# A two-layer token-mixer kernel on one core: preparation distance, bank emptying and bias place in the stage of seven block products

## The chip, the core and the metric

The kernel runs on 1 core of one Trainium2 chip. Its engines are TensorE (PE in the profile, with its weight loads as PEld), VectorE (DVE), ScalarE (ACT), GpSimd (POOL) and SyncE (SP), which issues most DMAs. The metric is device time in microseconds (us) of one launch, here the median of the runs shown.

## The reference

Two layers. In each, h = RMSNorm(x), one wide projection of h feeds four branches (pooling, latent attention, short convolution, attention into memory tokens), each branch is projected back, weighted by a sigmoid gate that also comes from h, and the sum goes through an output projection onto x. All is fp32; the sequence has 256 rows and the model 2048 columns. The stage that the change touches computes these pieces of it:

```
proj = h @ w_in[l]
(pv, pz, cq, ckv, kr, mz, cb, cc, cx, cz, xq, xz, gpre) = jnp.split(proj, split_points, axis=-1)
y_pool = pool_mixer(pv, pool_w[l], pool_scale[l]) * jax.nn.silu(pz)
y_conv = conv_mixer(cb, cc, cx, conv_w[l]) * jax.nn.silu(cz)
gates = jax.nn.sigmoid((gpre + gate_b[l]).astype(jnp.float32)).astype(x.dtype).reshape(B, S, N_BRANCH, D_MODEL)
```

pool_mixer takes causal window means of pv in four groups and multiplies each group by a 256x256 matrix; conv_mixer is cb times a three-tap causal convolution of cc * cx.

## The kernel before

**Number format.** Every fp32 weight is split on the chip into two parts that TensorE takes in one pass each: `hi`, a rounded copy made by ACT, and `lo`, the remainder, a subtraction on DVE. A weight chunk of 128 x 1024 therefore means a DMA into a `raw` tile (4 buffers), a cast into `hi` (5 buffers) and a subtraction into `lo` (5 buffers). The activations were split in the same way earlier (`op` tiles).

**The stage.** In each layer, after the gates of the mla and mem branches and before those of the pool and conv branches, `pool_branch` and `conv_branch` run on "fine" blocks (`fine_block`, L367 on): 128 output features, two weight chunks of 8 row blocks, per chunk 8 matmuls of 512 columns (L376: hi against the activations' hi and lo at once) and 8 of 256 (L379: lo against hi). A block gathers in one bank of PSUM, `ms`, 128 x 512: the main sum in its left half, the part from the activations' lo in its right half. There are two `ms` buffers. `fine_sum` empties the bank: ACT copies the right half into `fmt` (L384), DVE adds left half and copy (L385). There are 48 such blocks a layer; `pool_branch` also has 8 small tiles (L337, L338) of four matmuls, in the same `ms` buffers and emptied by the same `fine_sum`.

**The stream of products.** Between the blocks run three groups a layer of "seven block products" (`seven`, L413 on): a gate projection of 256 rows and 1024 columns done as seven half-size products instead of eight, with sums of weight quarters (L454, L455, L464, L465 on DVE) against sums of activation quarters made earlier (`sx`). A group walks over 8 pairs of row blocks. Each pair loads two `raw` tiles (L444), makes four hi/lo pairs (casts L446, L453, L463, L473; subtractions L438) and issues seven products of three matmuls (L429 to L431). They gather in seven banks: six in three `acc` tiles, the seventh in an `ms` tile that the group holds throughout, so that the blocks have the other `ms` buffer alone. After the last pair, DVE combines the banks (L482 to L489), adds the bias `gate_b` and ACT takes the sigmoid (L491 to L495); the result goes to DRAM as `kept` until `gates` fetches it.

**What interleaves them.** `seven` is a generator that yields after each product. `fine_block` first calls `pull(RATE)`, with RATE = 160/46 = 3.48 owed turns, and each pool tile `pull(1)`; `pull` takes whole turns from the first generator. A turn that gives True (a group is finished) ends the pull. `drain` takes what is left at the stage's end.

**What sets the order.** Instructions are written out in Python; a list scheduler then orders each engine's queue by priority, that is, place of writing, among what its own model of time holds ready, and gives out buffers in that order. `tc.high_priority(AHEAD)` lifts an instruction by 100 places: the DMA, cast and subtraction of a weight chunk then stand ahead of work written up to 100 places earlier. On the chip each engine works through its queue in that fixed order and waits where an input is missing.

Of the kernel before, what the change touches and what calls it, by code (L numbers as in the profile page):

```python
# [14 lines left out]
ALU = mybir.AluOpType  # L15
AX = mybir.AxisListType

P = 128
AHEAD = 100
PB = 2  # L20
D_H, D_MEM, D_LAT, D_XQ, D_MT = 4, 4, 6, 4, 3
SEQUENCE = "A0 A1 F T0 F T1 S0 A2 F V0 T2 S1 A3 F V1 T3 S2 F V2 S3 F V3 X0 X1 F Y0 Y1 X2 X3 F Y2 Y3"
# [4 lines left out]
S = 256  # L27
# [94 lines left out]
def tile_hybrid_trunk(  # L122
# [3 lines left out]
    V, A, T = nc.vector, nc.scalar, nc.tensor  # L126
# [28 lines left out]
    def t2(s):  # L155
        return tp.tile([P, 512], F32, tag="t2", name=nm(s), bufs=7)
# [145 lines left out]
    def defer(runs, delay):  # L302
        if len(background) < delay:
            background.extend([None] * (delay - len(background)))
        background.extend(runs)

    def wchunks(l, name, c0):
        off, n, nk, kt = plan[name, c0]
        m = nk * n
        for k0 in range(0, kt, nk):  # L310
            raw = wp.tile([P, 1024], F32, tag="raw", name=nm("raw"), bufs=4)
            hi = wp.tile([P, 1024], F32R, tag="hi", name=nm("hi"), bufs=5)
            lo = wp.tile([P, 1024], F32R, tag="lo", name=nm("lo"), bufs=5)
            o = off + P * n * k0
            step()
            with tc.high_priority(AHEAD):
                nc.sync.dma_start(raw[:, :m], weights[l, o : o + P * m].rearrange("(p m) -> p m", p=P))
                A.copy(hi[:, :m], raw[:, :m])  # L318
                V.tensor_tensor(lo[:, :m], raw[:, :m], hi[:, :m].bitcast(F32), ALU.subtract)  # L319
            yield k0, nk, kt, n, *(w[:, :m].rearrange("p (k n) -> p k n", n=n) for w in (hi, lo))  # L320
# [29 lines left out]
                    T.matmul(ps[:, j, :S], lo[:, k, n0 : n0 + P], o, start=False, stop=k0 + k == kt - 1)  # L350
        return ps

    stream, owed = [], [0.0]

    def pull(n):
        owed[0] += n
        while stream and owed[0] >= 1:
            owed[0] -= 1
            done = next(stream[0], True)
            if done:  # L360
                stream.pop(0)
                break

    def drain():
        while stream:
            owed[0] = 1000.0
            pull(0)  # L367
        owed[0] = 0.0
# [11 lines left out]
        return ps  # L380

    def fine_sum(dst, ps):
        tmp = t2("fmt")[:, :S]
        A.copy(tmp, ps[:, S:])  # L384
        V.tensor_tensor(dst, ps[:, :S], tmp, ALU.add)  # L385

    def fine_pair(dst, h, l, c0):
        for j in range(2):
# [23 lines left out]
    def seven(l, bi, ep, h, sx):  # L412
# [5 lines left out]
        for u in range(8):  # L418
# [19 lines left out]
                V.tensor_tensor(x[1][:, cols], raw[:, cols], x[0][:, cols].bitcast(F32), ALU.subtract)  # L438

            ra, rb = (wp.tile([P, 1024], F32, tag="raw", name=nm("raw"), bufs=4) for _ in range(2))  # L440
            with tc.high_priority(AHEAD):
                for i, r in enumerate((ra, rb)):
                    at = off + P * 1024 * (2 * u + i)
                    nc.sync.dma_start(r, weights[l, at : at + P * 1024].rearrange("(p m) -> p m", p=P))  # L444
                x = pair()
                A.copy(x[0][:, left], ra[:, left])  # L446
                lower(x, ra, left)
            product(1, "A11", x, left)
            yield False
            both = slice(0, 1024)  # L450
            with tc.high_priority(AHEAD):
                x = pair()
                A.copy(x[0], rb)  # L453
                V.tensor_tensor(ra[:, left], ra[:, right], ra[:, left], ALU.subtract)  # L454
                V.tensor_tensor(ra[:, right], rb[:, right], ra[:, right], ALU.subtract)  # L455
                lower(x, rb, both)
# [1 line left out]
            yield False  # L458
            product(2, "A12", x, left)
            yield False  # L460
            with tc.high_priority(AHEAD):
                x = pair()
                A.copy(x[0], ra)  # L463
                V.tensor_tensor(rb[:, right], rb[:, right], ra[:, left], ALU.subtract)  # L464
                V.tensor_tensor(rb[:, left], rb[:, right], rb[:, left], ALU.subtract)  # L465
                lower(x, ra, both)
# [1 line left out]
            yield False  # L468
            product(7, "S3", x, right)
            yield False  # L470
            with tc.high_priority(AHEAD):
                x = pair()
                A.copy(x[0], rb)  # L473
                lower(x, rb, both)
# [12 lines left out]
        V.tensor_tensor(c, c, bank[5], ALU.add)  # L487
        V.tensor_tensor(g[1][:, 0, :], c, bank[3], ALU.add)
        V.tensor_tensor(g[0][:, 1, :], u3, bank[4], ALU.subtract)  # L489
        for i in range(2):  # L490
            gb = tp.tile([P, 512], F32, tag="gb", name=nm("gb"), bufs=2)  # L491
            nc.sync.dma_start(gb, bcast_rows(gate_b[l, c0 + 512 * i : c0 + 512 * (i + 1)]))
            V.tensor_tensor(g[i], g[i], gb.unsqueeze(1).broadcast_to([P, 2, 512]), ALU.add)
            A.activation(g[i], g[i], AF.Sigmoid)
            nc.gpsimd.dma_start(kept[bi, 2 * ep + i], g[i])  # L495
        yield True

    def fm_sum(dst, ps):
        tmp = t2("fmt").rearrange("p (n s) -> p n s", n=2)
# [92 lines left out]
    def mem_operands(gt):  # L592
# [3 lines left out]
        def get(i):  # L596
            if i not in made:
                f0 = 2 * i
                mt = t2("mt").rearrange("p (k s) -> p k s", k=2)
                made[i] = opnd()  # L600
                with tc.high_priority(AHEAD):
                    if i == 0:
# [119 lines left out]
    def xattn_scores(hd, xq, rq, kT):  # L722
# [6 lines left out]
        for t in range(2):  # L729
            for n in range(2):  # L730
# [3 lines left out]
                )  # L734
        pb = tp.tile([P, 512], F32, tag="pb", name=nm("pb"), bufs=PB)
        softmax_rows(ps, pb, ((0, S), (S, 2 * S)), rq[hd], 2)
# [294 lines left out]
    for l in range(DEPTH):  # L1031
# [51 lines left out]
        flush()  # L1083
        stream += [seven(l, bi, ep, h, sx) for bi, ep in SEVEN]
        owed[0] = -RATE
        y_pool = pool_branch(l, vec, h)
        y_conv = conv_branch(l, vec, h)
        drain()
        gates(l, h, y_pool, "pool", False, False)
        mT = gates(l, h, y_conv, "conv", False, True)  # L1090
        if l + 1 < DEPTH:
# [66 lines left out]
```

## Time and profile before

| what | us |
|---|---|
| median of 3 runs | 2582.64 (2579.9 to 2584.72) |
| the profiled execution's own time | 2583.21 |
| its span | 2581.4 |
| the stage in layer 0 | 629 to 1069 of the span |
| the stage in layer 1 | 1912 to 2353 of the span |

Times in the views count from the start of the span. A matmul's row is longer than its distance to the next one, since matmuls are pipelined; the distance from start to start is what PE needs. In a list of waits, "PEld acc L429 <- ACT hi L446" reads: the weight load of line 429 for `acc` waited for the cast of line 446. The granted clock (PEclk) is TensorE's, 1.00 at full speed.

### The profile page before, as it was taken

Reading aid. Unit: us, or ns where it says so; the run is one execution under the profiler, and the core shown is the slowest. Engines: PE = TensorE matmul, PEld = TensorE weight load, DVE = VectorE, ACT = ScalarE, POOL = GpSimd, SP = SyncE. Lnnn points to the kernel's source line nnn. Section 1 sums busy time; section 2 is a strip of 40 time slices with the busy share of each in tenths; the row PEclk is TensorE's granted clock in tenths of the full one; section 3 lists DMA queues with packets and bytes.
Section 4 is the critical chain, followed back from the end, with each engine's and each line's share of the span. In section 5 each row is a group of like instructions: output and inputs, shape, how many; then the busy total and the mean of one; then the engine's idle time right before and its main releaser. Section 6 shows DMA issues by size and latency. Waiting matters only on the chain.

```text
span 2581.4 us, 33256 instructions
## 1 busy us (share of the span) xinstructions
PE 2511.1 (97%) x12258; PEld 2091.0 (81%) x12258; DVE 1799.0 (70%) x2646; ACT 1338.9 (52%) x1881; POOL 40.5 (2%) x88
## 2 busy tenths in 40 slices
PE   8999999999998999999999999999999999899999
PEld 6888888888877878888888888888888778788887
DVE  6767786556878878766574577965568777777653
ACT  7556674444545455445454566744445454544442
POOL 0000000000000000000000000000000000001000
PEclk9999999999999999999999999999999999999999
DMA  8665436676545565776655653466765455567764
GB/s 310 214 205 164 142 128 222 225 236 219 183 162 187 174 214 189 267 294 232 218 186 162 202 170 123 147 220 226 232 210 188 163 188 193 186 201 273 257 228 147
DMA packets 154052, 522.03 MB, mean 202 GB/s; under 512 B 17312, under 2 KB 18336, under 8 KB 153888
## 3 DMA queue, kind: packets, MB, share of 16 engines
q1 hardware_dynamic: 142800, 481.06, 56.8%
q0 software_dynamic: 10368, 37.75, 4.0%
q8 instruction: 96, 1.57, 0.2%
q10 hardware_dynamic: 720, 1.09, 0.1%
q14 instruction: 68, 0.56, 0.1%
HBM read 496.76 MB, written 23.07 MB: 201 GB/s over the span
## 4 chain that ended last, share of the span: by engine, by line
PE 88%; DVE 6%; DMA 2%; ACT 2%; issue 1%; SPq 0%; DVEq 0%; ACTq 0%
PE acc L333 18%; PE acc L332 18%; PE acc L331 18%; PE ms L376 13%; PE ms L379 6%; PE acc L347 4%; PE acc L350 2%; DVE lo L319 2%; DMA raw<-in_weights_dram 2%; PE acc L430 2%; PE acc L429 2%; PE acc L431 2%; DVE lo L438 1%; ACT hi L318 1%; PE ms L870 1%
## 5 line engine op out<-in xcount | busy, mean ns | idle before, releaser
L319 DVE TENSOR_TENSOR lo<-raw,hi 128x1024 fp32r<-128x1024 f32 (+1 forms) x788 | 942.6, 1199 | 579.7 <-ACT hi L318 572.3
L318 ACT CAST hi<-raw 128x1024 fp32r<-128x1024 f32 (+1 forms) x788 | 812.1, 1033 | 879.9 <-PE acc L333 586.5
L331 PE MATMUL acc<-hi,op 128*128 128x512 f32 (+2 forms) x2112 | 812.5, 385 | 6.0 <-ACT op L555 5.7
L332 PE MATMUL acc<-lo,op 128*128 128x512 f32 (+2 forms) x2112 | 808.0, 383 | 1.6 <-DVE lo L319 1.6
L333 PE MATMUL acc<-hi,op 128*128 128x512 f32 (+2 forms) x2112 | 808.5, 383 | 0.5 <-DVE op L556 0.5
L331 PEld LDWEIGHTS acc<-hi,op 128*128 128x128 f32 x2112 | 396.9, 188 | 79.8 <-ACT op L555 6.4
L333 PEld LDWEIGHTS acc<-hi,op 128*128 128x128 f32 x2112 | 396.7, 188 | 77.8 <-issue 1.3
L332 PEld LDWEIGHTS acc<-lo,op 128*128 128x128 f32 x2112 | 397.0, 188 | 76.0 <-DVE lo L319 2.8
L376 PE MATMUL ms<-op,hi 128*128 128x512 f32 x1536 | 400.6, 404 | 10.6 <-DVE z L385 7.0
L376 PEld LDWEIGHTS ms<-op,hi 128*128 128x128 f32 x1536 | 289.8, 195 | 79.2 <-DVE z L385 10.8
L438 DVE TENSOR_TENSOR lo<-raw,hi 128x512 fp32r<-128x512 f32 x192 | 208.5, 1089 | 96.5 <-PE ms L379 26.4
L379 PEld LDWEIGHTS ms<-op,lo 128*128 128x128 f32 x1536 | 210.9, 191 | 15.7
L379 PE MATMUL ms<-op,lo 128*128 128x256 f32 x1536 | 214.7, 283 | 0.0
L347 PE MATMUL acc<-op,hi 128*128 128x512 f32 x512 | 144.3, 397 | 0.0
L347 PEld LDWEIGHTS acc<-op,hi 128*128 128x128 f32 x512 | 87.6, 189 | 11.7 <-issue 0.7
L453 ACT CAST hi<-raw 128x1024 fp32r<-128x1024 f32 x48 | 50.4, 1051 | 82.4 <-PE ms L376 49.7
L350 PEld LDWEIGHTS acc<-op,lo 128*128 128x128 f32 x512 | 78.5, 189 | 10.7 <-issue 0.7
L430 PE MATMUL acc<-lo,sx 128*128 128x512 f32 x192 | 78.9, 411 | 8.3 <-DVE lo L438 8.0
L429 PE MATMUL acc<-hi,sx 128*128 128x512 f32 x192 | 77.5, 405 | 8.4 <-ACT hi L473 6.4
L350 PE MATMUL acc<-op,lo 128*128 128x256 f32 x512 | 83.8, 283 | 0.0
L431 PE MATMUL acc<-hi,sx 128*128 128x512 f32 x192 | 75.6, 394 | 0.0
L463 ACT CAST hi<-raw 128x1024 fp32r<-128x1024 f32 x48 | 50.5, 1051 | 44.6 <-PE ms L376 30.7
(254 smaller groups left out, 1990.4 us busy)
## 6 DMA issues: line engine op xcount, KB each, us to landing
raw<-in_weights_dram SPq DMA_DIRECT2D x836, 512.0 KB, 4.2
sums<-g POOLq DMA_DIRECT2D x24, 512.0 KB, 5.3
mg<-sums POOLq DMA_DIRECT2D x24, 512.0 KB, 7.9
raw<-in_weights_dram SPq DMA_DIRECT2D x32, 288.0 KB, 2.8
gb<-in_gate_b_dram SPq DMA_DIRECT2D x32, 256.0 KB, 4.2
raw<-in_weights_dram SPq DMA_DIRECT2D x16, 384.0 KB, 3.0
kept<-g POOLq DMA_DIRECT2D x12, 512.0 KB, 6.9
g<-kept POOLq DMA_DIRECT2D x12, 512.0 KB, 6.6
```

The lines of the kernel that those rows point to most:

```text
L318: A.copy(hi[:, :m], raw[:, :m])
L319: V.tensor_tensor(lo[:, :m], raw[:, :m], hi[:, :m].bitcast(F32), ALU.subtract)
L331: T.matmul(ps[:, t, :n], hh, hi[:, k, :], start=kk == 0, stop=False)
L332: T.matmul(ps[:, t, :n], hh, lo[:, k, :], start=False, stop=False)
L333: T.matmul(ps[:, t, :n], hl, hi[:, k, :], start=False, stop=kk == kt - 1)
L347: T.matmul(ps[:, j, :], hi[:, k, n0 : n0 + P], o, start=k0 + k == 0, stop=False)
L350: T.matmul(ps[:, j, :S], lo[:, k, n0 : n0 + P], o, start=False, stop=k0 + k == kt - 1)
L376: T.matmul(ps, hi[:, k, :], o, start=k0 + k == 0, stop=False)
L379: T.matmul(ps[:, :S], lo[:, k, :], o, start=False, stop=k0 + k == kt - 1)
L429: T.matmul(bank[i], lh[0], hi[:, cols], start=u == 0, stop=False)
L430: T.matmul(bank[i], lh[0], lo[:, cols], start=False, stop=False)
L438: V.tensor_tensor(x[1][:, cols], raw[:, cols], x[0][:, cols].bitcast(F32), ALU.subtract)
```

## The change

Three edits, all for that stage.

1. A cell `lead` holds the number of places by which weight preparation is lifted. It is 100 (AHEAD) outside the stage and 40 (NEAR) from just before `pool_branch` until after `drain`. `wchunks` and `seven` use it.
2. `fine_sum` copies the whole bank, 128 x 512, by ACT into `fmt`, and the add on DVE reads both halves from there. DVE no longer reads the `ms` bank.
3. In `seven`, `yield True` stands ahead of the bias, sigmoid and store. They run in the group's next turn, which issues no product and then ends the generator; `pull` now drops a generator when it is exhausted and not when it gives True.

```diff
@@ -17,6 +17,7 @@
 
 P = 128
 AHEAD = 100
+NEAR = 40
 PB = 2
 D_H, D_MEM, D_LAT, D_XQ, D_MT = 4, 4, 6, 4, 3
 SEQUENCE = "A0 A1 F T0 F T1 S0 A2 F V0 T2 S1 A3 F V1 T3 S2 F V2 S3 F V3 X0 X1 F Y0 Y1 X2 X3 F Y2 Y3"
@@ -304,6 +305,8 @@
             background.extend([None] * (delay - len(background)))
         background.extend(runs)
 
+    stream, owed, lead = [], [0.0], [AHEAD]
+
     def wchunks(l, name, c0):
         off, n, nk, kt = plan[name, c0]
         m = nk * n
@@ -313,7 +316,7 @@
             lo = wp.tile([P, 1024], F32R, tag="lo", name=nm("lo"), bufs=5)
             o = off + P * n * k0
             step()
-            with tc.high_priority(AHEAD):
+            with tc.high_priority(lead[0]):
                 nc.sync.dma_start(raw[:, :m], weights[l, o : o + P * m].rearrange("(p m) -> p m", p=P))
                 A.copy(hi[:, :m], raw[:, :m])
                 V.tensor_tensor(lo[:, :m], raw[:, :m], hi[:, :m].bitcast(F32), ALU.subtract)
@@ -350,15 +353,15 @@
                     T.matmul(ps[:, j, :S], lo[:, k, n0 : n0 + P], o, start=False, stop=k0 + k == kt - 1)
         return ps
 
-    stream, owed = [], [0.0]
 
     def pull(n):
         owed[0] += n
         while stream and owed[0] >= 1:
             owed[0] -= 1
-            done = next(stream[0], True)
+            done = next(stream[0], None)
+            if done is None:
+                stream.pop(0)
             if done:
-                stream.pop(0)
                 break
 
     def drain():
@@ -380,9 +383,9 @@
         return ps
 
     def fine_sum(dst, ps):
-        tmp = t2("fmt")[:, :S]
-        A.copy(tmp, ps[:, S:])
-        V.tensor_tensor(dst, ps[:, :S], tmp, ALU.add)
+        tmp = t2("fmt")
+        A.copy(tmp, ps)
+        V.tensor_tensor(dst, tmp[:, :S], tmp[:, S:], ALU.add)
 
     def fine_pair(dst, h, l, c0):
         for j in range(2):
@@ -438,7 +441,7 @@
                 V.tensor_tensor(x[1][:, cols], raw[:, cols], x[0][:, cols].bitcast(F32), ALU.subtract)
 
             ra, rb = (wp.tile([P, 1024], F32, tag="raw", name=nm("raw"), bufs=4) for _ in range(2))
-            with tc.high_priority(AHEAD):
+            with tc.high_priority(lead[0]):
                 for i, r in enumerate((ra, rb)):
                     at = off + P * 1024 * (2 * u + i)
                     nc.sync.dma_start(r, weights[l, at : at + P * 1024].rearrange("(p m) -> p m", p=P))
@@ -448,7 +451,7 @@
             product(1, "A11", x, left)
             yield False
             both = slice(0, 1024)
-            with tc.high_priority(AHEAD):
+            with tc.high_priority(lead[0]):
                 x = pair()
                 A.copy(x[0], rb)
                 V.tensor_tensor(ra[:, left], ra[:, right], ra[:, left], ALU.subtract)
@@ -458,7 +461,7 @@
             yield False
             product(2, "A12", x, left)
             yield False
-            with tc.high_priority(AHEAD):
+            with tc.high_priority(lead[0]):
                 x = pair()
                 A.copy(x[0], ra)
                 V.tensor_tensor(rb[:, right], rb[:, right], ra[:, left], ALU.subtract)
@@ -468,7 +471,7 @@
             yield False
             product(7, "S3", x, right)
             yield False
-            with tc.high_priority(AHEAD):
+            with tc.high_priority(lead[0]):
                 x = pair()
                 A.copy(x[0], rb)
                 lower(x, rb, both)
@@ -487,13 +490,13 @@
         V.tensor_tensor(c, c, bank[5], ALU.add)
         V.tensor_tensor(g[1][:, 0, :], c, bank[3], ALU.add)
         V.tensor_tensor(g[0][:, 1, :], u3, bank[4], ALU.subtract)
+        yield True
         for i in range(2):
             gb = tp.tile([P, 512], F32, tag="gb", name=nm("gb"), bufs=2)
             nc.sync.dma_start(gb, bcast_rows(gate_b[l, c0 + 512 * i : c0 + 512 * (i + 1)]))
             V.tensor_tensor(g[i], g[i], gb.unsqueeze(1).broadcast_to([P, 2, 512]), ALU.add)
             A.activation(g[i], g[i], AF.Sigmoid)
             nc.gpsimd.dma_start(kept[bi, 2 * ep + i], g[i])
-        yield True
 
     def fm_sum(dst, ps):
         tmp = t2("fmt").rearrange("p (n s) -> p n s", n=2)
@@ -1083,9 +1086,11 @@
         flush()
         stream += [seven(l, bi, ep, h, sx) for bi, ep in SEVEN]
         owed[0] = -RATE
+        lead[0] = NEAR
         y_pool = pool_branch(l, vec, h)
         y_conv = conv_branch(l, vec, h)
         drain()
+        lead[0] = AHEAD
         gates(l, h, y_pool, "pool", False, False)
         mT = gates(l, h, y_conv, "conv", False, True)
         if l + 1 < DEPTH:
```

The lines below are as built; lines of the kernel after stand three or more further down than before (L385 is L388, L438 is L441). Numbers behind a name are the tile's; tiles of one number in hi and lo belong together.

**Conv branch, layer 0: the block of bank `ms1445`, near 867 us.** PE before, the last twelve products' matmuls ahead of the next block: S3, S2, A22 (into `ms1316`) and then A11 of the next pair, whose weights are hi1481 and lo1482.

```order
L429 MATMUL acc1314_6967<-hi1467_7760,sx719_3800 128x512
L430 MATMUL acc1314_6967<-lo1468_7761,sx719_3800 128x512
L431 MATMUL acc1314_6967<-hi1467_7760,sx719_3800 128x512
L429 MATMUL acc1313_6966<-hi1469_7772,sx719_3800 128x512
L430 MATMUL acc1313_6966<-lo1470_7773,sx719_3800 128x512
L431 MATMUL acc1313_6966<-hi1469_7772,sx719_3800 128x512
L429 MATMUL ms1316_6969<-hi1469_7772,op144_736 128x512
L430 MATMUL ms1316_6969<-lo1470_7773,op144_736 128x512
L431 MATMUL ms1316_6969<-hi1469_7772,op144_736 128x512
L429 MATMUL acc1313_6966<-hi1481_7834,op149_762 128x512
L430 MATMUL acc1313_6966<-lo1482_7835,op149_762 128x512
L431 MATMUL acc1313_6966<-hi1481_7834,op149_762 128x512
```

PE after: S2 of the same pair (hi1469), the end of the block of `ms1471`, which now stands behind S2, and then A22 and the next pair's A11. Twelve of the block's sixteen rows are left out between the two pieces.

```order
L432 MATMUL acc1315_6974<-hi1469_7772,sx719_3800 128x512
L433 MATMUL acc1315_6974<-lo1470_7773,sx719_3800 128x512
L434 MATMUL acc1315_6974<-hi1469_7772,sx719_3800 128x512
L379 MATMUL ms1471_7779<-op110_573,hi1473_7781 128x512 x2
L379 MATMUL ms1471_7779<-op124_632,hi1473_7781 128x512 x2
```

and, behind the block's other rows,

```order
L382 MATMUL ms1471_7779<-op149_762,lo1477_7804 128x256 x2
L382 MATMUL ms1471_7779<-op154_788,lo1477_7804 128x256 x2
L432 MATMUL ms1318_6977<-hi1469_7772,op144_736 128x512
L433 MATMUL ms1318_6977<-lo1470_7773,op144_736 128x512
L434 MATMUL ms1318_6977<-hi1469_7772,op144_736 128x512
L432 MATMUL acc1315_6974<-hi1481_7834,op149_762 128x512
L433 MATMUL acc1315_6974<-lo1482_7835,op149_762 128x512
L434 MATMUL acc1315_6974<-hi1481_7834,op149_762 128x512
```

What moved: a block of 32 matmuls now stands between S2 and A22, and A11 follows A22 behind it. Before, seven products and A11 followed each other without a block.

DVE before, at the same place. hi1481 is the next pair's first cast, `ms1445` the bank of the block just done.

```order
L958 SCALAR_TENSOR_TENSOR cc1336_7045<-u1389_7328,gt0_93,cc1336_7045 128x256
L319 TENSOR_TENSOR lo1474_7785<-raw1472_7783,hi1473_7784 128x1024
L959 SCALAR_TENSOR_TENSOR cc1336_7045<-u1389_7328,gt0_93,cc1336_7045 128x256
L319 TENSOR_TENSOR lo1477_7807<-raw1475_7805,hi1476_7806 128x1024
L438 TENSOR_TENSOR lo1482_7835<-raw1479_7830,hi1481_7834 128x512
L385 TENSOR_TENSOR cb1440_7617<-ms1445_7640,fmt1452_7685 128x256
L454 TENSOR_TENSOR raw1479_7830<-raw1479_7830 128x512
```

ACT after, at the same place: `ms1445` and the next block's `ms1459` are copied whole.

```order
L321 CAST hi1464_7732<-raw1463_7731 128x1024
L387 COPY fmt1452_7682<-ms1445_7637 128x512
L466 CAST hi1467_7760<-raw1453_7688 128x1024
L476 CAST hi1469_7772<-raw1454_7689 128x1024
L321 CAST hi1473_7781<-raw1472_7780 128x1024
L321 CAST hi1476_7803<-raw1475_7802 128x1024
L387 COPY fmt1466_7753<-ms1459_7708 128x512
L449 CAST hi1481_7834<-raw1479_7830 128x512
L456 CAST hi1483_7841<-raw1480_7831 128x1024
```

What moved: before, the add that frees `ms1445` stood on DVE behind the next pair's lo1482. After, that bank is free with ACT's copy, ahead of the casts L466 and L476, and the next bank's copy stands ahead of the next pair's first cast (hi1481).

**Pool branch, layer 0: the small tiles, near 741 us.** PE before: two tiles (`ms1243`, `ms1245`) follow each other.

```order
L430 MATMUL ms1064_5746<-lo1266_6733,op149_762 128x512
L431 MATMUL ms1064_5746<-hi1265_6732,op149_762 128x512
L337 MATMUL ms1243_6624<-op1110_5974,hi1230_6577 128x512
L338 MATMUL ms1243_6624<-op1110_5974,lo1231_6578 128x256
L337 MATMUL ms1243_6624<-op1110_5974,hi1230_6577 128x512
L338 MATMUL ms1243_6624<-op1110_5974,lo1231_6578 128x256
L337 MATMUL ms1245_6635<-op1110_5974,hi1230_6577 128x512
L338 MATMUL ms1245_6635<-op1110_5974,lo1231_6578 128x256
L337 MATMUL ms1245_6635<-op1110_5974,hi1230_6577 128x512
```

PE after, the tiles `ms1237` and `ms1243`.

```order
L340 MATMUL ms1237_6603<-op1080_5822,hi1230_6577 128x512
L341 MATMUL ms1237_6603<-op1080_5822,lo1231_6578 128x256
L340 MATMUL ms1237_6603<-op1080_5822,hi1230_6577 128x512
L341 MATMUL ms1237_6603<-op1080_5822,lo1231_6578 128x256
L434 MATMUL ms1064_5746<-hi1241_6617,op144_736 128x512
L432 MATMUL acc1061_5743<-hi1251_6653,op149_762 128x512
L433 MATMUL acc1061_5743<-lo1252_6654,op149_762 128x512
L434 MATMUL acc1061_5743<-hi1251_6653,op149_762 128x512
L340 MATMUL ms1243_6624<-op1110_5974,hi1230_6577 128x512
L341 MATMUL ms1243_6624<-op1110_5974,lo1231_6578 128x256
L340 MATMUL ms1243_6624<-op1110_5974,hi1230_6577 128x512
L341 MATMUL ms1243_6624<-op1110_5974,lo1231_6578 128x256
```

What moved: there is now a product (into `acc1061`) between these tiles.

## The prediction

> **What bounds the kernel now.** First the page's busy shares, then a table of stretches, with each layer's stage cut at the end of its pool branch. The columns are length, then busy time and instruction count of PE, PEld, DVE, ACT and POOL, then granted clock, DMA share and GB/s.
>
> ```profile
> PE 2511.1 (97%) x12258; PEld 2091.0 (81%) x12258; DVE 1799.0 (70%) x2646; ACT 1338.9 (52%) x1881; POOL 40.5 (2%) x88
> ```
> ```profile
> 629.00:806.00 177.00, 161.87 (x792) 130.83 (x791) 146.74 (x190) 91.61 (x117) 2.03 (x7) 0.96 0.55 181
> 806.00:1069.00 263.00, 249.41 (x1280) 208.17 (x1281) 208.06 (x260) 131.11 (x157) 2.82 (x6) 0.98 0.59 192
> 1912.00:2089.50 177.50, 162.73 (x795) 131.83 (x795) 147.83 (x190) 92.13 (x118) 2.04 (x7) 0.96 0.54 181
> 2089.50:2353.00 263.50, 250.53 (x1276) 208.62 (x1275) 207.15 (x259) 131.12 (x157) 2.81 (x6) 0.97 0.58 192
> 743.01:749.84 6.83, 6.06 (x14) 4.24 (x15) 4.68 (x9) 2.46 (x4) 0.00 (x0) 0.50 0.29 92
> 872.72:876.13 3.41, 3.21 (x8) 2.53 (x9) 2.65 (x5) 1.04 (x1) 0.00 (x0) 0.50 0.77 270
> 1019.49:1971.00 951.51, 948.68 (x4634) 796.44 (x4634) 628.40 (x949) 499.62 (x726) 16.62 (x34) 1.00 0.62 206
> ```
>
> Between the two stages PE idles 2.8 of 951.5 us at full clock: nothing is to be had there. In the stages PE loses in two ways: it idles (15.1, 13.6, 14.8 and 13.0 us in the four stretches), and its clock stands at half for pieces of 3.41 us, such as the one from 872.72. The mean clock prices the second: 177 x 0.04 + 263 x 0.02 + 177.5 x 0.04 + 263.5 x 0.03 = 27 us.
>
> How fast would the stage be with neither loss? The timeline of an undisturbed place tells, by start against start (the 0.39 us rows overlap their successors):
>
> ```profile
> 652.93 0.39 PE L430 MATMUL acc<-lo,op 128*128 128x512 f32 x1
> 653.15 0.39 PE L431 MATMUL acc<-hi,op 128*128 128x512 f32 x1
> 653.38 1.98 PE L376 MATMUL ms<-op,hi 128*128 128x512 f32 x8
> 655.20 1.11 PE L379 MATMUL ms<-op,lo 128*128 128x256 f32 x8
> 656.15 2.00 PE L376 MATMUL ms<-op,hi 128*128 128x512 f32 x8
> 657.99 1.12 PE L379 MATMUL ms<-op,lo 128*128 128x256 f32 x8
> 658.94 0.40 PE L429 MATMUL acc<-hi,sx 128*128 128x512 f32 x1
> ```
>
> A fine block takes 658.94 - 653.38 = 5.56 us, a 512-wide matmul 0.225, a product of three 0.675; a 256-wide one 0.95 / 8 = 0.119, so a pool tile of two and two 0.69. A layer has 48 blocks, 168 products and 8 tiles: 266.9 + 113.4 + 5.5 = 386 us, against 440 and 441 measured. **The loss is about 54 us a layer, 109 in all**, half of it in the pool stretch (177 us, where 16 blocks, 8 tiles and 83 products need 150) and half in the conv stretch (263 against 235).
>
> What is waited for? Here is the list of waits, PE's weight loads alone (sum us, times, longest), first the conv stretch of layer 0, then four rows of its pool stretch:
>
> ```profile
> PEld acc L430 <- DVE lo L438: 6.6, 11, 2.4
> PEld acc L429 <- ACT hi L446: 6.1, 3, 2.4
> PEld ms L376 <- DVE z L385: 3.7, 3, 2.0
> PEld ms L376 <- DVE cc L385: 1.9, 2, 1.1
> PEld acc L429 <- ACT hi L473: 1.7, 1, 1.7
> PEld ms L376 <- DVE cb L385: 1.6, 2, 0.8
> PEld acc L429 <- DVE c L487: 0.9, 1, 0.9
> ```
> ```profile
> PEld acc L430 <- DVE lo L438: 5.8, 8, 1.1
> PEld acc L429 <- ACT hi L446: 5.6, 3, 3.2
> PEld ms L337 <- DVE yp L385: 3.1, 2, 2.2
> PEld ms L376 <- DVE z L385: 1.7, 2, 0.9
> ```
>
> There are two kinds: L385 rows wait for the small bank `ms` to be emptied by the DVE add, the others for a product's weights, hi or lo. In conv they make 7.2 and 14.4 us. The largest conv place, on the timeline:
>
> ```profile
> 867.02 2.12 SPq L444 DMA_DIRECT2D raw<-in_weights_dram  x2
> 871.52 0.62 ACT L446 CAST hi<-raw 128x512 fp32r<-128x512 f32 x1 [1.72 <-DMA raw<-in_weights_dram]
> 872.17 0.69 DVE L438 TENSOR_TENSOR lo<-raw,hi 128x512 fp32r<-128x512 f32 x1 [0.33 <-ACT hi L446]
> 872.20 0.51 PE L429 MATMUL acc<-hi,op 128*128 128x512 f32 x1 [1.93 <-ACT hi L446]
> 872.78 0.42 DVE L385 TENSOR_TENSOR cb<-ms,fmt 128x256 f32<-128x256 f32 x1
> ```
>
> Seven products ran without a block between. The eighth belongs to the next 128-row pair, whose DMA (867.02) needed 4.5 us before its cast. The block that could have filled the gap needs `ms`, and its emptying add stands on DVE behind that very lo (872.17 before 872.78). One late transfer thus stops both streams, and the clock halves in the next piece, 872.72 to 876.13.
>
> **The change, part by part.**
>
> *Emptying the bank.* The groups of ACT and DVE, forms apart (sum us, mean ns):
>
> ```profile
> L384 ACT COPY fmt<-ms 128x256 f32<-128x256 f32 x112 | 41.5, 370 | 12.5 <-PE ms L379 8.6 <-PE ms L338 3.8
> L482 ACT COPY c<-acc 128x512 f32<-128x512 f32 x6 | 3.5, 583 | 0.0
> L400 DVE TENSOR_TENSOR sw<-op 128x256 f32<-128x256 f32 x16 | 6.7, 419 | 0.0
> L493 DVE TENSOR_TENSOR g<-g,gb 128x1024 f32<-128x1024 f32 x12 | 14.1, 1216 | 0.0
> ```
>
> 112 copies go from 370 to 583 ns (L482 is the same form out of PSUM): 24 us more on ACT, 12 in each 440 us stage where it is busy 223. The add keeps its 0.42 us (L400 is the form with both operands in SBUF). The bank comes free after 0.58 us of one engine instead of 0.37 + 0.42 us plus whatever DVE has queued. Three products between blocks last 2.03 us, so an emptying that starts within 1.4 us of a block's end is hidden. If that cover goes, the block waits for the rest. In conv I let the L385 waits go from 7.2 to 0.7: **-6.5 a layer**. In pool, where a tile of 0.69 us alternates with products, I take 4.0 of the 4.8 in its two rows: **-4.0**. This place shows why; DVE does a split (L505) while PE needs the add:
>
> ```profile
> 742.22 0.68 DVE L505 TENSOR_TENSOR op<-yp,op 128x512 fp32r<-128x512 f32 x1
> 742.82 0.42 DVE L385 TENSOR_TENSOR yp<-ms,fmt 128x256 f32<-128x256 f32 x1
> 743.29 0.79 PE L337 MATMUL ms<-op,hi 128*128 128x512 f32 x1 [1.84 <-DVE yp L385]
> ```
>
> *Forty places instead of 100, and the order that results.* No instruction is added. The rows of order show conv going from runs of eight products to a steady three and four, with a block in front of each next pair's first product. That block gives the transfer 5.56 us more, over its 4.5; and ACT empties a block before the next pair's cast. So of the 14.4 us of product waits I keep 4.1 (the 1.7 row and one wait of 2.4, which lie where one group gives its banks to the next), and 1.0 more for mishaps: **-9.3 a layer**. In pool I count nothing: DVE is busy 146.7 us where PE needs 150, so weights stay late there.
>
> What bounds this term? Below, all 14.4 stay; above, all go. I stand nearer the upper end because DVE in conv has 208 us of work in 235.
>
> *The clock.* Half-speed pieces follow pieces in which PE idled some 2 us. Conv loses 263 x 0.02 and 263.5 x 0.03, on average 6.6 a layer; with its waits gone I let 5.5 go. In pool the pair 743.01 to 749.84 follows the `ms` wait above: 6.83 / 2 = 3.4 goes, the rest stays. **-8.9 a layer.**
>
> The trace shows halves after idling far short of a whole piece: 1.93 us of PE before 872.72. The Trainium skill, "TensorE: Matmul & The Clock Gate", Part 1 (the HAM clock gate), has a free-running window of about 3.4 us, as here, but lets the clock fall only after at least one idle window. By that rule no wait in the lists (longest 3.2) causes a half, and the 8.9 would stay.
>
> *The bias a step later.* Twelve adds (1.22 us), twelve sigmoids, their loads and stores move behind the next pull, so each group uses one turn that issues no product: three turns more a layer. The products then last until before the last block, where before none ran (part of the 2.0 us z wait, already counted). The gb loads move by a few DMA rows on SP, the stores to `kept` go by POOL, which is busy 40.5 us. Cost nothing, hidden behind blocks of 5.56; uncovered, 2.4 us of DVE a group, 15 us in all.
>
> Sum a layer: 6.5 + 4.0 + 9.3 + 8.9 = 28.7; both 57.4. From the profiled execution's own 2583.2 (span 2581.4 and 1.8 around it): **2525.8 us**. The median of the runs shown is 2582.6, so the same against that.
>
> **The rivals.**
>
> *Nearly all goes.* If the pool stretch comes within 12 us of its 150 and conv within 1 of its 235, about 42 a layer: 2583 - 85 = 2498. For it: all pieces of the loss hang together through the clock. Against it: DVE's 146.7.
>
> *Only the bank waits go.* The product waits and most halves stay, since DVE work and transfers are unchanged: 2 x (6.5 + 4.0 + 2) = 25, 2558. For it: lo L438 is the longest row.
>
> *The halves stay* though the waits go, for a cause of their own: 2583.2 - 2 x 19.8 = 2543.6. Against it: the 951 us between the stages, without waits, have none.
>
> *It doesn't do what it says.* The emptying copies now stand behind casts that wait for a transfer, and PE waits for ACT where it waited for DVE: within 0.2% (5 us, about what a measurement of this kernel can tell from no change), 2583.
>
> *Slower: the late cast blocks the bank.* ACT works in order. Where the first cast of the next pair stands ahead of an emptying copy and its transfer is late, every block behind it waits. A layer has 24 pairs, and today's loss is 109 / 48 = 2.3 us a pair; the change loses as soon as the new wait per pair exceeds that. With 40 places of lead, DVE's elementwise work gets in front of the lo's that free the raw buffers, which makes transfers later. At 3.1 us a pair (a 4.5 us transfer less 1.4 of cover) the time is 2583 + 48 x 0.8 = 2621. For it: only four raw buffers, two held by each pair. Against it: in conv's order after the change most emptying copies come first.
>
> **How the numbers follow.** Forecast (2510 to 2545) 0.52; nearly all 0.12; only the bank 0.14; halves stay 0.04; no effect 0.07; slower 0.11. The range 2498 to 2575 leaves out the last two, 0.18. Faster 0.82, same 0.07, slower 0.11.
>
> **What would show it.** The stages' lengths, 440 before, should be 411 or so, conv losing more than pool (about 242 and 170). In the waits of the loads L385 should be gone as releaser, and the copy of `fmt` should hold under 2 us a layer. The copy should take 583 ns, the add 418. The clock of conv should be 0.99 or 1.00. The forecast is wrong if the lo L438 row grows, if `fmt` takes the place of the L385 rows at the same sum, or if the halves stay while waits shrink.

## The result and the profile after

The kernel after takes 2508.32 us (median of 4 runs, 2505.73 to 2509.94) against 2581.27 for the kernel before (2578.95 to 2584.72): **73 us less, ratio 0.9715, 95% interval 0.9699 to 0.9732**. The forecast was 2526 with a range of 2498 to 2575. The direction was right and the time lies in the range, but the gain is 73 us where 57 were forecast. Times here and below are medians; one of the four runs of e_bank below took 4200.43 us at a mean granted clock of 0.59 and is left out of its median.

The page's busy shares after, first PE:

```profile
PE 2473.0 (99%) x12258; PEld 2080.0 (83%) x12258; DVE 1790.1 (71%) x2646; ACT 1356.9 (54%) x1881; POOL 40.4 (2%) x88
```

DVE's busy time is 8.9 us less than before and ACT's 18 us more, on 73 us of time: the gain is hardly work saved. Next the table of stretches, with the columns used in the prediction, each layer's stage cut at its last pool tile. The prediction's cuts, 806 and 2089.5, lie some 15 us behind that tile, so its stretches are not quite these; the row of before by this cut (162.60 us in the pool stretch of layer 0) stands below, where the prediction is compared.

```profile
629.00:770.40 141.40, 138.14 (x731) 117.74 (x729) 126.79 (x168) 84.47 (x102) 2.03 (x7) 1.00 0.57 190
770.40:1031.40 261.00, 255.20 (x1347) 216.83 (x1347) 222.56 (x282) 148.26 (x175) 2.81 (x6) 1.00 0.65 213
1875.80:2017.80 142.00, 137.95 (x729) 117.51 (x727) 126.91 (x167) 84.87 (x102) 2.04 (x7) 1.00 0.57 190
2017.80:2277.00 259.20, 255.00 (x1346) 216.84 (x1346) 221.57 (x279) 148.48 (x174) 2.81 (x6) 1.00 0.64 213
```

The clock is 1.00 in all four; before it was 0.96 to 0.98. From the start of the stage's first fine matmul to the start of its last, a stage takes 401.7 and 400.9 us; before it took 439.9 and 440.7. That is 78 us less in the two stages, and the spans differ by 77.4 (2581.4 and 2504.0). Against the 386 us of work, 16 are still lost in a layer, of 54.

The list of waits of PE's weight loads after, layer 0, first the conv stretch, then the pool stretch (sum us, times, longest):

```profile
PEld ms L379 <- ACT fmt L387: 6.2, 8, 1.8
PEld acc L433 <- DVE lo L441: 3.1, 4, 1.4
PEld ms L379 <- ACT hi L321: 1.6, 1, 1.6
```
```profile
PEld ms L340 <- ACT fmt L387: 2.2, 4, 1.6
PEld acc L433 <- DVE lo L441: 2.0, 1, 2.0
PEld acc L432 <- ACT hi L476: 0.8, 1, 0.8
PEld ms L379 <- ACT fmt L387: 0.2, 1, 0.2
```

DVE's add is gone as a releaser, but the copy stands in its place with 8.6 us. What nearly vanished is the other kind: loads that wait for a product's weights make 3.1 + 2.0 + 0.8 = 5.9 us. Before, the same list over the whole stage of layer 0 has them at the top:

```profile
PEld acc L430 <- DVE lo L438: 12.4, 19, 2.4
PEld acc L429 <- ACT hi L446: 11.7, 6, 3.2
PEld ms L376 <- DVE z L385: 5.4, 5, 2.0
PEld acc L429 <- ACT hi L473: 4.5, 4, 1.7
PEld ms L337 <- DVE yp L385: 3.1, 2, 2.2
PEld ms L376 <- DVE cc L385: 1.9, 2, 1.1
PEld ms L376 <- DVE cb L385: 1.6, 2, 0.8
```

The three rows of `acc` make 28.6 us, the four of `ms` 12.0. A load can wait while PE still works on the matmul ahead of it, so these sums are somewhat larger than PE's idling.

The place that the prediction showed, a pair's transfer and first cast in the conv branch, on the timeline after (start, duration):

```profile
862.71 1.46 SPq L447 DMA_DIRECT2D raw<-in_weights_dram  x2
864.31 2.00 PE L379 MATMUL ms<-op,hi 128*128 128x512 f32 x8
867.31 0.59 ACT L387 COPY fmt<-ms 128x512 f32<-128x512 f32 x1
868.00 0.62 ACT L449 CAST hi<-raw 128x512 fp32r<-128x512 f32 x1
```

The transfer (862.71) now runs beside a block, the cast (868.00) waits for nothing, and the bank is copied ahead of it. Before, that cast waited 1.72 us for its transfer and PE 1.93 us for the cast.

### The profile page after: what moved, and what is told of

Its sections match the earlier page's. It is cut to its first block, busy times and chain, and to the rows that moved or that the text cites. A ratio compares the mean times of both kernels' runs of the same rounds, so it can differ in the third digit from the quotient of the medians.

```text
span 2504.0 us, 33197 instructions
## 1 busy us (share of the span) xinstructions
PE 2473.0 (99%) x12258; PEld 2080.0 (83%) x12258; DVE 1790.1 (71%) x2646; ACT 1356.9 (54%) x1881; POOL 40.4 (2%) x88
## 4 chain that ended last, share of the span: by engine, by line
PE 84%; DVE 7%; DMA 5%; ACT 2%; issue 1%; SPq 0%; DVEq 0%; ACTq 0%
PE acc L336 18%; PE acc L335 18%; PE acc L334 18%; PE ms L379 10%; DMA raw<-in_weights_dram 5%; PE ms L382 5%; PE acc L350 4%; PE acc L353 2%; DVE lo L322 2%; PE acc L433 2%; PE acc L432 2%; PE acc L434 2%; DVE lo L441 1%; ACT hi L321 1%; PE ms L873 1%
## 5 line engine op out<-in xcount | busy, mean ns | idle before, releaser
L379 PE MATMUL ms<-op,hi 128*128 128x512 f32 x1536 | 384.9, 392 | 6.7 <-ACT fmt L387 4.8
L379 PEld LDWEIGHTS ms<-op,hi 128*128 128x128 f32 x1536 | 280.8, 188 | 68.2 <-ACT fmt L387 12.3
L441 DVE TENSOR_TENSOR lo<-raw,hi 128x512 fp32r<-128x512 f32 x192 | 206.3, 1088 | 28.2 <-ACT hi L449 12.8
L387 ACT COPY fmt<-ms 128x512 f32<-128x512 f32 x112 | 65.0, 580 | 6.3 <-PE ms L382 5.9
L456 ACT CAST hi<-raw 128x1024 fp32r<-128x1024 f32 x48 | 50.4, 1051 | 33.1 <-DMA raw<-in_weights_dram 15.4
```

Of the source, the lines that this page charges most:

```text
L379: T.matmul(ps, hi[:, k, :], o, start=k0 + k == 0, stop=False)
```

## The experiments

The theories at the start: **S**, each edit takes its own waits, so that the gains add up; **O**, order: PE must not meet seven or more products in a row, since the eighth belongs to a pair whose weights are not there yet, and any edit that puts a block there takes the same loss; **L**, the lead alone does it; **B**, the bias work weighs more than forecast. PE's queue, read as a string of blocks and products over both layers, has eight runs of eight or nine products before, and none longer than four after.

| kernel | edits | us | ratio to before, 95% interval | runs of 8 or 9 |
|---|---|---|---|---|
| e_bank | 2 | 2516.18 | 0.9753, 0.9737 to 0.9769 | 0 |
| e_lead | 1 | 2527.76 | 0.9797, 0.9781 to 0.9814 | 0 |
| e_bias | 3 | 2560.22 | 0.9925, 0.9910 to 0.9940 | 6 |
| e_lead_bank | 1, 2 | 2506.01 | 0.9715, 0.9701 to 0.9730 | 0 |
| e_bank_bias | 2, 3 | 2514.97 | 0.975, 0.9731 to 0.9768 | 0 |
| e_turn | 3, turn only | 2564.59 | 0.994, 0.9919 to 0.996 | 6 |
| e_move | 3, move only | 2578.94 | 0.9989, 0.9977 to 1.0001 | 8 |
| e_lift_before | none, emptying lifted | 2511.19 | 0.9729, 0.9715 to 0.9744 | 0 |
| e_lift_add | none, add lifted | 2523.62 | 0.9783, 0.9766 to 0.9799 | 0 |
| e_dve_bank | none, bank copied by DVE | 2594.41 | 1.0052, 1.0036 to 1.0069 | 8 |
| e_near85 | 1 to 3, 85 places | 2521.2 | 0.9775, 0.9756 to 0.9794 | 0 |
| e_best | 1, 2, copy lifted | 2506.23 | 0.9707, 0.9693 to 0.9722 | 0 |

The kernel before took 2578.93, 2582.44, 2581.07 and 2580.11 us (medians) beside them.

### Each edit alone, and the first two

e_bank is before with the second edit:

```diff
-        tmp = t2("fmt")[:, :S]
-        A.copy(tmp, ps[:, S:])
-        V.tensor_tensor(dst, ps[:, :S], tmp, ALU.add)
+        tmp = t2("fmt")
+        A.copy(tmp, ps)
+        V.tensor_tensor(dst, tmp[:, :S], tmp[:, S:], ALU.add)
```

> Edit 2 alone on the kernel before (whole bank copied by ScalarE; 100 places, bias at its old place). Theory S (the two kinds of waits go by their own edits, and add up): only the bank waits go, 6.5 + 4.0 a layer, with the pool pair of half-speed pieces, 3.4, and one conv piece, 1.7: 2 x 15.6 = 31 us, about 2550. Theory O (what counts is that no run of eight products without a block is left, and edit 2 or edit 1 alone does that): 50 to 65 us, 2517 to 2532, and no half-speed piece left in the conv stretch. Theory L (the lead of 40 places does it): under 15 us, above 2566.

e_lead is before with the first edit. The first pair of lines stands once in `wchunks` and four times in `seven`; the definitions of NEAR and `lead` are left out.

```diff
-            with tc.high_priority(AHEAD):
+            with tc.high_priority(lead[0]):
...
+        lead[0] = NEAR
         y_pool = pool_branch(l, vec, h)
         y_conv = conv_branch(l, vec, h)
         drain()
+        lead[0] = AHEAD
```

> Edit 1 alone (40 places; bank emptied by ScalarE and VectorE as before). Theory S: the product waits of conv and their half-speed pieces go, 9.3 + 3.8 a layer, 26 us, about 2555, and the L385 waits stay at 7 us in conv. Theory O: 50 to 65 us, 2517 to 2532, since its order too has runs of five or six products at most. Theory L: 60 us or more, under 2521.

e_bias is before with the third edit, `pull` included (its lines are shown under e_turn):

```diff
+        yield True
         for i in range(2):
...
-        yield True
```

> Edit 3 alone (bias, sigmoid and store in a turn of their own). Theories S, O and L: its order keeps runs of eight and nine products, so the product waits stay; only the z wait of 2.0 us before each stage's last block goes, with the one half-speed piece behind it: 4 to 6 us, 2575 to 2579. A theory B (two bias adds of 1.22 us ahead of the lo's are what makes PE wait where groups meet): 15 us or more, under 2566.

e_lead_bank is after with the third edit taken back, in `pull` too (not shown):

```diff
-        yield True
         for i in range(2):
...
+        yield True
```

> Edits 1 and 2 without 3. Theory S: what edits 1 and 2 give alone adds up, and the whole change less some 5 us is reached, about 2513. Theory O: hardly better than the better of the two alone, within 10 us of it. Theory B: at least 15 us slower than the whole change, 2523 or more.

Alone, the edits give 63, 51 and 19 us, together 133; the whole change gives 73. So they don't add up, and S's sizes fail (it had 2550 and 2555 for the first two). Either of the first two edits does most of the whole, as O said, and the two together reach the time of the whole change: the third adds nothing to them. They lie 10 us under e_bank, at the edge of what O allowed. L fails by e_bank. For e_bias only B had the number, which O didn't explain.

Two things don't fit O as it stood. It said that no half-speed piece would be left in e_bank's conv stretch, and two are (from 920.89 and 2030.22). And e_lead, with no run longer than five, still has 16.6 us of waits for a product's weights in layer 0, 9.5 of them in three waits for a pair's first cast (L448 there, up to 4.0 us). So to be rid of the long runs is most of the gain, but not all of it.

### What of the third edit gains alone

e_turn keeps the bias in its old place, with only `pull` changed, so that each group ends in a turn that issues no product:

```diff
-            done = next(stream[0], True)
+            done = next(stream[0], None)
+            if done is None:
+                stream.pop(0)
             if done:
-                stream.pop(0)
                 break
```

> Before, with the third edit's extra turn only: a finished group still adds its bias, takes its sigmoid and stores in the old place, and its generator ends in a turn that issues no product. Theory T (turn): the 18.7 us of edit 3 alone came from the three empty turns a layer, which shift the products against the blocks, so that two runs of eight products a layer lie elsewhere and a product stands in front of the last block; TensorE's order here is nearly that of edit 3 alone, so 2555 to 2566. Theory M (move): it came from the bias work leaving the place between the combination of one group and the next group's first pair; then nothing is gained here, 2575 to 2582.

e_move is e_bias with that turn given back:

```diff
             if done is None:
                 stream.pop(0)
+                owed[0] += 1
```

> Before, with the third edit's move only: bias, sigmoid and store run one pull later, but the turn in which they run is given back, so that the number of products per pull is as before. Theory T: 2575 to 2582, no gain, since TensorE's order of products and blocks is nearly that of before (six runs of eight and two of nine in both). Theory M: 2555 to 2566. If both parts carry some of it, both kernels lie between, near 2570.

The turn alone gives the gain, 18 us beside the 18.7 of e_bias, and the move none that can be measured. The bias work was rightly costed at nothing, and B falls. The empty turn shifts the products against the blocks and leaves six long runs of eight: 9 us for each run less. At that price all eight runs make 72 us, about the whole gain, which agrees with O and does not prove it: the kernels without long runs lie anywhere from 51 (e_lead) to 75 us (e_best) under before, 6 to 9 us a run.

> The second and third edits without the first (100 places). Alone they gave 62 and 19 us. If the third edit's gain is a gain of order (theory O), it is for the most part the same microseconds, the runs of eight products that the second edit has broken up already: 2510 to 2519. If it is work taken out of the way (theories B and M), it adds up: 2495 to 2501.

e_bank_bias, the second and third edits, lies within 2 us of e_bank: the third edit's gain is the same loss taken once, as O had it.

### The order without any edit

e_lift_before leaves all three edits out and lifts the emptying of the bank in the scheduler's order:

```diff
-        tmp = t2("fmt")[:, :S]
-        A.copy(tmp, ps[:, S:])
-        V.tensor_tensor(dst, ps[:, :S], tmp, ALU.add)
+        with tc.high_priority(100):
+            tmp = t2("fmt")[:, :S]
+            A.copy(tmp, ps[:, S:])
+            V.tensor_tensor(dst, ps[:, :S], tmp, ALU.add)
```

> Before, with none of the three edits: the bank is emptied by ScalarE's half copy and VectorE's add as it was, but both are lifted by 100 places, like the weight preparation, so that they are not put behind it. TensorE's order has no run of more than five products then (before: six runs of eight and two of nine). Theory O (order: what the change gains is that the emptying no longer stands behind the next pair's preparation, by whichever way): 2512 to 2530, without any edit of the change. Theory Q (engine: VectorE must be rid of the bank, since its queue is full): a small part only, 2550 to 2575, with the waits for the add (L387) still at over 4 us a layer.

It takes 2511.19 us: 70 of the 73 us, with the same instructions as before and only another order. Its pool stretch in layer 0, cut at the last pool tile, and the waits of the weight loads in the whole stage of layer 0:

```profile
631.80:774.80 143.00, 139.26 (x730) 117.50 (x729) 127.14 (x165) 80.14 (x103) 0.84 (x4) 1.00 0.58 192
```
```profile
PEld ms L376 <- DVE cc L386: 4.3, 3, 2.1
PEld ms L376 <- DVE z L386: 3.0, 5, 1.6
PEld ms L376 <- DVE yp L386: 1.8, 2, 1.1
PEld acc L431 <- DVE lo L439: 1.8, 2, 0.9
PEld ms L337 <- DVE yp L386: 1.7, 2, 1.2
PEld acc L430 <- ACT hi L474: 1.6, 1, 1.6
PEld ms L337 <- DVE z L386: 1.5, 2, 0.9
```

Here is the surprise. The five rows of `ms` make 12.3 us, as much as the four of before (12.0). **The waits for the emptying did not shrink, and the time fell by 70 us all the same.** What fell are the product rows, from 28.6 to 3.4 us, and the clock's half pieces, from 23.9 us to 3.4 in this layer. Theory Q (VectorE must be rid of the bank) said that waits of over 4 us would stay, which they did, and that little would be gained, which fails.

e_dve_bank is the counterpart: one engine frees the bank, but the wrong one, and PE's order keeps its long runs.

```diff
-        tmp = t2("fmt")[:, :S]
-        A.copy(tmp, ps[:, S:])
-        V.tensor_tensor(dst, ps[:, :S], tmp, ALU.add)
+        tmp = t2("fmt")
+        V.tensor_copy(tmp, ps)
+        V.tensor_tensor(dst, tmp[:, :S], tmp[:, S:], ALU.add)
```

> Before, with the whole bank copied by VectorE in place of ScalarE, the add from the copy: one engine frees the bank, as after the second edit, but it is the engine that also makes the lo's. TensorE's order keeps runs of seven to nine products. Theory C (chain: what counts is that the bank needs one engine and not two): 2550 to 2570. Theories O and Q: no gain or a loss, 2580 to 2620, since the emptying still stands behind the lo's and VectorE has 112 longer rows.

It is half a per cent slower than before, 1.0052. The stretches of layer 0, cut at the last pool tile, and the first waits of its weight loads:

```profile
632.10:798.30 166.20, 152.42 (x747) 123.57 (x745) 148.85 (x199) 79.11 (x85) 2.03 (x7) 0.96 0.55 180
798.30:1078.40 280.10, 265.10 (x1329) 220.29 (x1330) 231.62 (x303) 130.19 (x136) 2.82 (x6) 0.95 0.58 188
```
```profile
PEld acc L430 <- DVE lo L438: 15.1, 15, 2.8
PEld acc L429 <- ACT hi L446: 9.8, 6, 2.5
PEld acc L429 <- ACT hi L473: 4.9, 4, 2.2
```

The product rows stay (29.8 us), and the clock stays at 0.96 and 0.95. So one engine in place of two is not enough, and C's 2550 to 2570 does not come. This run alone can't rule out a smaller gain of that kind, because it also gives DVE 112 copies of 685 ns. But e_lift_before gains 70 us with two engines, so the gain doesn't need one. What ScalarE's copy does, by these two runs, is to take the emptying from behind the lo's in the order, and the next block with it.

e_lift_add lifts the add alone:

```diff
         A.copy(tmp, ps[:, S:])
-        V.tensor_tensor(dst, ps[:, :S], tmp, ALU.add)
+        with tc.high_priority(100):
+            V.tensor_tensor(dst, ps[:, :S], tmp, ALU.add)
```

> Before, with VectorE's add alone lifted by 100 places; ScalarE's half copy stays where it was written, behind weight preparation that is lifted past it. Theory O1 (the add behind the lo's on VectorE is the step that matters): most of the 70 us of the kernel with both lifted, 2508 to 2525. Theory O2 (the copy behind the casts on ScalarE matters as much): half of it or less, 2535 to 2565.

It gives 56.5 us, O1's case: the add's place behind the lo's makes four fifths of e_lift_before's gain. Lifting the copy on top of it gives the other 13; the copy lifted alone wasn't run.

### Is 40 the number?

e_near85 is after with another lead:

```diff
-NEAR = 40
+NEAR = 85
```

> The whole change with 85 places of lead in place of 40. Theory N (distance: the less the lead, the less weight preparation stands ahead of the emptying): 85 lies three quarters of the way back to 100, so 2512 to 2517. Theory O (order: all that counts is how TensorE's order comes out, and 85, 70, 50, 30 and 10 places give one and the same order of products and blocks, close to that of 40): 2502 to 2512, the same as the whole change within what can be measured.

Neither theory has its 2521.2 us. PE's order of products and blocks is that of after but for places among the pool's small tiles and the blocks next to them, and no run is longer than four; yet it is about 14 us slower, even a little above e_bank_bias with its 100 places. Much of the loss lies in the pool stretch, in layer 0 147.3 us where after has 141.4, as the table of stretches has it:

```profile
628.60:775.90 147.30, 141.54 (x735) 118.90 (x733) 131.78 (x172) 87.50 (x106) 2.03 (x7) 0.99 0.59 195
```

Rows of ACT and PE at its end:

```profile
769.59 0.62 ACT L449 CAST hi<-raw 128x512 fp32r<-128x512 f32 x1 [1.31 <-DVE lo L322]
770.65 0.57 ACT L387 COPY fmt<-ms 128x512 f32<-128x512 f32 x1
771.27 0.50 PE L340 MATMUL ms<-op,hi 128*128 128x512 f32 x1 [0.51 <-ACT fmt L387]
777.46 3.50 PE L379 MATMUL ms<-op,hi 128*128 128x512 f32 x8 [0.98 <-ACT fmt L387]
```

The next pair's first cast (769.59) stands ahead of the copy (770.65) and waits 1.31 us itself; the tile behind (771.27) waits for the copy, and the clock is at half from 773.67 to 780.50 (eight matmuls in 3.50 us, where they take 2.0). In the stages of the two layers it has 17 us at half speed, worth 8.5, and after has none; its weight loads wait 13.0 us for copies in layer 0, those of after 8.6. So O has to be widened: ACT's order of casts against copies counts too, and at this place the longer lead puts a cast ahead. That this order, and not PE's at the small tiles, makes the 14 us was not tested. Whether 10 or 20 places do as well as 40 wasn't tried.

### A version that beats both?

e_best is e_lead_bank with the copy lifted:

```diff
-        A.copy(tmp, ps)
+        with tc.high_priority(100):
+            A.copy(tmp, ps)
```

> The first two edits, with the whole-bank copy on ScalarE lifted by 100 places too. The waits for the copy of the bank, 5.4 us in a layer after the whole change and 3.8 us with the first two edits, come from copies that stand behind casts. If the lift takes most of them and moves nothing else: 2500 to 2504, about 2 to 5 us under the first two edits alone. If it only moves the waits to the casts, which then come later: 2505 to 2511, the same.

At 2506.23 us it is the same as the whole change and as e_lead_bank. Its waits show why: the copy's rows stay, at 7.8 us (8.6 in the whole change, 6.5 with the first two edits; the 5.4 and 3.8 of the expectation are not these sums), and a cast comes late.

```profile
PEld ms L378 <- ACT fmt L387: 4.6, 8, 1.9
PEld ms L340 <- ACT fmt L387: 3.2, 6, 1.4
PEld acc L432 <- ACT hi L449: 2.4, 1, 2.4
```

No version here beats the whole change by more than can be measured.

## Why the prediction was right in direction and short by 16 us

**The floor and the kinds of loss** were right: 386 us of work in a stage, and both stages together give up 78 of their 109 us of loss.

**Emptying the bank: mis-sized, too high.** The durations hold, the copy at 580 ns (583 forecast) and the add at 419 (418):

```profile
L387 ACT COPY fmt<-ms 128x512 f32<-128x512 f32 x112 | 65.0, 580 | 6.3 <-PE ms L382 5.9 <-PE ms L341 0.3
L388 DVE TENSOR_TENSOR z<-fmt 128x256 f32<-128x256 f32 x32 | 13.4, 419 | 0.0
```

But the `ms` waits were to lose 6.5 + 4.0 = 10.5 us a layer. The four rows of 12.0 became three of 8.6, so they lost 3.4. "Under 2 us a layer" for the copy failed, and the sign of being wrong that `fmt` takes the place of the L385 rows came half true. The timeline of after shows why at one of these waits: the copy (944.69) stands behind three casts, of which the first two waited for transfers.

```profile
941.30 1.05 ACT L321 CAST hi<-raw 128x1024 fp32r<-128x1024 f32 x1 [3.50 <-DMA raw<-in_weights_dram]
942.79 1.05 ACT L321 CAST hi<-raw 128x1024 fp32r<-128x1024 f32 x1 [0.44 <-DMA raw<-in_weights_dram]
943.75 1.04 ACT L456 CAST hi<-raw 128x1024 fp32r<-128x1024 f32 x1
944.69 0.58 ACT L387 COPY fmt<-ms 128x512 f32<-128x512 f32 x1
945.32 2.11 PE L379 MATMUL ms<-op,hi 128*128 128x512 f32 x8 [1.40 <-ACT fmt L387]
```

And e_lift_before reached nearly the whole gain with this term at nothing.

**Product waits: right in kind in conv, the step that failed in pool.** In pool the prediction counted nothing: "DVE is busy 146.7 us where PE needs 150, so weights stay late there." Its count for that stretch was off to begin with (up to 806 there are 17 blocks and 70 products, 148 us, not 16 and 83). Here is the pool stretch of before once more, now cut at the last pool tile as after, with its three rows of product waits:

```profile
629.00:791.60 162.60, 151.04 (x743) 123.06 (x742) 136.21 (x176) 83.33 (x107) 2.03 (x7) 0.96 0.54 180
```
```profile
PEld acc L429 <- ACT hi L446: 5.6, 3, 3.2
PEld acc L430 <- DVE lo L438: 4.7, 7, 1.1
PEld acc L429 <- ACT hi L473: 1.3, 2, 1.0
```

These make 11.6 us, and after 2.0 + 0.8 = 2.8 are left: 8.8 us a layer that the sum didn't have. In conv, the rest of the 28.6, 17.0, became 3.1: 13.9 us, where 9.3 were forecast. DVE's time was not what held pool up. It was busy 136.21 of 162.60 us, 84%; after, it is busy 126.79 of 141.40, 90%, and keeps up. That the pool's waits hang on the order is shown by e_lift_before, whose pool stretch takes 143.00 us by the same cut with the instructions of before; which of its places does it was not taken apart. For the same reason the sign "conv losing more than pool" did not come: by this cut pool became 21 us shorter (162.60 to 141.40) and conv 17 (278.4 to 261.00).

**The clock: right in mechanism, mis-sized.** 8.9 us a layer were forecast; the half pieces of the two stages, 23.9 and 27.3 us, are all gone, worth 12.0 and 13.7. The rest in pool, which was to stay, went with the pool's product waits. So the rival *halves stay* has fallen. By the rule that the prediction took from the Trainium skill, "TensorE: Matmul & The Clock Gate", Part 1 (the HAM clock gate), the clock falls only after a whole idle window; here the trace decides against it, as the last section shows.

**The bias step** was costed at nothing, and on top of the first two edits it is nothing (e_lead_bank and the whole change have the same ratio, 0.9715). Alone it gains, by its empty turn.

**The sum.** Of 28.7 us a layer, the `ms` waits gave 7 less, and the product waits 13 more (9 of it in pool), the clock 3 to 5 more. For layer 0 that makes 3.4 + 22.7 + 12.0 = 38 us, what its stage lost (38.2). That they agree so well is partly luck: the load waits overlap PE's work, and PE's own listed waits fell by less, from 28.4 to 9.0 us. What the prediction's form missed is that the terms are not separate: it priced each wait at its row, where one order causes the waits and the halves together. The measured 2508 lies between *nearly all goes* (2498) and the forecast (2526), 10 us from the one and 17 from the other, just outside the 2510 to 2545 that had the chance of 0.52. Pool met the rival's condition (start to start it loses 5 us of the 12 allowed), conv did not (11 us where 1 was allowed). *Slower: the late cast blocks the bank* is a real mechanism, seen at 944.69 above and in e_near85, but smaller than the gain; *it doesn't do what it says* fell with it.

## What to carry to other kernels

Before pricing each wait by its own row, look for the place in the queue that causes several of them: here runs of eight products, which outran a transfer of 4.5 us, cost about 6 to 9 us each by the estimate above, while the waits for the emptying that stood beside them in the list could stay (12.3 us in e_lift_before) and 70 us went. Test an order by itself, with lifted priorities and no other edit, before crediting the edit that changed it. A busy share of 84% on an engine that feeds another is no proof that it is the bound: see whether it idles while it is late.

## What the runs showed of the hardware

The clock falls to half after a partly idle piece, with a sharp border. For this, the stages of all traces that have half pieces were cut into the 3.41 us pieces in which the clock moves, and for each piece the distances between PE's matmul starts beyond 0.225 us (512 columns) and 0.119 us (256) were added up. The clock fell 76 times. Of the 72 pieces at full speed with 2.10 us or more of such idling, 71 were followed by a half; of some 2870 with less than 1.99 us none was; of the 17 between, 5 were. The longest idling in one piece was 3.28 us, so none of the 76 falls follows a wholly idle piece. Two pieces of before, with 1.97 and 2.60 us, each with the piece behind it:

```profile
794.21:797.62 3.41, 1.89 (x8) 0.91 (x6) 3.37 (x6) 2.07 (x3) 0.00 (x0) 1.00 0.75 226
797.62:801.04 3.42, 3.07 (x17) 2.68 (x18) 2.54 (x4) 1.60 (x3) 0.00 (x0) 1.00 0.83 236
...
1012.66:1016.08 3.42, 1.28 (x5) 0.48 (x3) 3.08 (x5) 1.00 (x2) 0.55 (x1) 1.00 0.78 241
1016.08:1019.49 3.41, 3.40 (x8) 2.72 (x9) 2.65 (x4) 1.04 (x1) 0.00 (x0) 0.50 0.93 332
```

The first stays at 1.00, the second goes to 0.50. PE's busy time in the rows is longer than 3.41 less this idling, since a matmul's row overlaps the next. By that border, an estimate from these pieces: two waits of 1.1 us in one piece cost 3.41 / 2 = 1.7 us more than in two pieces, and a wait that shrinks a little can take a half piece with it.
